# A hybrid decoder layer in fp32: the second mixer matrix with 14 pairs by products over halves, gate weights fetched a tile ahead, value products in one piece

## The chip, the core and the metric

The program runs on one core of one Trainium2 chip. Five engines take part: TensorE (PE, with its weight loads PEld), VectorE (DVE), ScalarE (ACT), GpSimd (POOL) and SyncE (SP). SP does nothing here but issue DMAs; a few are issued by POOL and ACT. Every engine works through its own instructions in a fixed order, and semaphores keep the engines in step. The metric is the time of one execution on the device in microseconds. Engine loads and stretches come from one profiled execution.

## What is computed

One inference step of a decoder layer for 1024 prompt tokens and 32 sample tokens (T = 1056), all in fp32:

```python
h = rmsnorm(x)
p = h @ w_in       # -> q, k, v | conv input | z | a | b | gate_A | gate_B
o_a = stick_breaking(q, k, v)          # 8 heads of 64, strictly causal, no softmax
o_b = gated_delta(conv(u), z, a, b)    # 4 heads, 128 x 128 state
m = sigmoid(gate_A) * (o_a @ w_pa) + sigmoid(gate_B) * (o_b @ w_pb)
x = x + m @ w_o
x = x + relu(rmsnorm(x) @ w_up)**2 @ w_down     # 1024 -> 4096 -> 1024
y = rmsnorm(x)
# stick_breaking: z = q.k/8 + bias; weight of key j =
#   sigmoid(z_j) * product over later keys l of (1 - sigmoid(z_l)); then weights @ v
```

The caches of keys and values, the convolution rows and the delta states are returned too.

## The kernel before

Every dense product is made of three matmuls in a single-pass fp32 format: each operand is split into a rounded part (`hi`, copied by ACT) and the rest (`lo`, subtracted by DVE), and `dense` (lines 134 to 139) issues hi by hi (L137), hi by lo (L138) and lo by hi (L139) into one PSUM tile. The weights come from device memory by DMA into a staging tile, and `load_w` (L117) or the like makes the two parts.

An automatic planner orders the instructions. It plays the program on a model of the engines and places on each engine, at each moment, a ready instruction, earlier lines of the program first; `tc.high_priority()` lifts what is inside, and `tc.issue_after(ins)` keeps what is inside behind `ins` on the engine of `ins`. The order so found is fixed in the program: on the chip each engine keeps to it, and waits where its next instruction isn't ready.

The stages, with their places in the profiled execution:

- Norm, input products, the delta heads and the sample tokens (0 to about 618 us). The 16 gate tiles (8 column tiles of 128 for gate_A and gate_B) are made by `gate_steps` (L1047), which calls `proj_steps` (L232): four steps, one for each of four pieces of the tokens; the first step loads the weight tile (`ws_g`, one staging buffer; `wh_g` and `wl_g`, two buffers each). Eleven gate tiles are written in the program before attention, five as filling inside it.
- Attention (about 618 to 869 us). Blocks are (head, i): 128 queries by 128(i+1) keys, 64 blocks, heads 6 and 7 taking turns at the end. `scores` makes z on PE (`sc`), the sigmoid on ACT, the causal mask (L951) and 1 - s (`am`, L954) on POOL, the running product (`pr`, a scan, L958) and its product with s (L959) on DVE. `stage_b` (L1030) then turns the weights by PE transposes (`wt`, L111) in PSUM, copies them out on ACT (L970), and `values_of` (L983) multiplies them by the values (`po`). For heads 0 to 5 two neighbouring blocks share one PSUM tile, one in rows 0 to 63 and one in rows 64 to 127, and the product of each step of 128 keys is issued for the one and then for the other, so `values_of` does something at odd i alone; heads 6 and 7 share one in the same way. Each value product takes 64 columns of the array and appears in the trace as two instructions. `pipeline` runs the scores LAG = 4 blocks ahead of the transposes and hands out the filling: the last five gate tiles and the transposes of x (`residual_step`) in the first 34 blocks, the products with w_pb (`pb_step`) in the other 30.
- Merge (`pa`) and output product with w_o (`px`), about 869 to 1008 us, then the norm ahead of the mixer.
- First mixer matrix (`pu`, about 1008 to 1350 us). The token columns are handled in two groups g. Of the 32 column tiles of w_up, tile f and tile f + 16 are a pair. A pair can be made plainly (`up_plain`, 8 row tiles deep), or with seven half-deep products over halves instead of eight (`up_weights`, `up_products`), which takes sums of weight quarters and of input quarters beforehand and sums of products behind. In group 0 the first NPL = 3 pairs are plain, which gives the input sums time to be made; all else goes by seven products.
- Second mixer matrix (`pw`, about 1350 to 1621 us). The hidden tiles f and f + 16 are a pair again. Pairs 3 to 15 go by seven products over halves, in three groups of 4, 4 and 5 pairs; `weight_part` (L1481) makes the weight sums and the hi and lo parts of each of the seven, `load_h` brings the hidden sums. Those were made at the end of `up_products` by four subtractions (L1410 to L1413) and written to `hc_d`, the squared hidden tiles of pairs 0 to 2 to `h_d`. For the first product of the first group the loads are issued by POOL, all the others by SP.
- Plain rest (`pv`, about 1621 to 1700 us): the six hidden tiles of pairs 0 to 2, in four stages of token columns, eight column tiles each, followed by the last norm, transposes (`fin`) and the stores.

Of the kernel before, what the change touches and what calls it, by code (L numbers as in the profile page):

```python
# [8 lines left out]
F32 = mybir.dt.float32  # L9
# [3 lines left out]
AF = mybir.ActivationFunctionType  # L13
ALU = mybir.AluOpType
# [4 lines left out]
P = 128  # L19
# [19 lines left out]
def hybrid_step(ctx, tc, x_prompt, x_sample, cache_k, cache_v, page_table, state_conv, state_ssm,  # L39
# [68 lines left out]
    V.memset(powc[:, 1:2], 0.5)  # L108

    def tr(out, in_, k=P):  # L110
        PE.transpose(out, in_, ident[:k, :k])  # L111

    def rpow(out, in_, which, n):
        G.tensor_tensor(out, in_, powc[: out.shape[0], which:which + 1].to_broadcast([out.shape[0], n]), op=ALU.pow)
# [114 lines left out]
                      [xhc[c][:, k] for k in range(KT)], [xlc[c][:, k] for k in range(KT)], n)  # L229
                evac(c, o, n, pt)  # L230

    def proj_steps(col, name, evac, done):  # L232
        ws = []

        def step(c, o, n):
            if not ws:
                ws.append(load_w(winv[:, :, col:col + P], name))
            wh, wl = ws[0]
            pt = dtile(f"pd_{name}_{c}", True)
            dense(pt, [wh[:, k] for k in range(KT)], [wl[:, k] for k in range(KT)],  # L240
                  [xhc[c][:, k] for k in range(KT)], [xlc[c][:, k] for k in range(KT)], n)
            evac(c, o, n, pt)
            if c == len(CX) - 1:
                done()

        return [lambda c=c, o=o, n=n: step(c, o, n) for c, (o, n) in enumerate(CX)]
# [692 lines left out]
    def scores(blk):  # L939
        hh, i = blk  # L940
        qs, kh, kl = heads[hh]
        n = P * (i + 1)
        qsl = slice(i * P, n)
        s = ak.tile([P, NP], F32, tag="s", name=f"s{hh}_{i}", bufs=LAG + 2)
        for k0 in range(0, n, 512):
            kn_ = min(512, n - k0)
            pt = dtile(f"sc{hh}_{i}_{k0}")
            PE.matmul(pt[:, :kn_], lhsT=qs[:, qsl], rhs=kh[:, k0:k0 + kn_], start=True, stop=False)
            last = PE.matmul(pt[:, :kn_], lhsT=qs[:, qsl], rhs=kl[:, k0:k0 + kn_], start=False, stop=True)
            S_.activation(s[:, k0:k0 + kn_], pt[:, :kn_], AF.Sigmoid, bias=sbb[:, hh:hh + 1], scale=HD ** -0.5)  # L950
        G.affine_select(s[:, qsl], s[:, qsl], pattern=[[-1, P]], compare_op=ALU.is_gt, fill=0.0, base=0,  # L951
                        channel_multiplier=1)
        am = ak.tile([P, NP], F32, tag="am", name=f"am{hh}_{i}", bufs=2)
        G.tensor_scalar(am[:, :n], s[:, :n], -1.0, 1.0, op0=ALU.mult, op1=ALU.add)  # L954

        pr = ak.tile([P, NP], F32, tag="pr", name=f"pr{hh}_{i}")
        am_r = am[:, n - 1:0:-1]
        V.tensor_tensor_scan(pr[:, n - 1:0:-1], am_r, am_r, 1.0, op0=ALU.mult, op1=ALU.bypass)  # L958
        V.tensor_tensor(s[:, :n - 1], s[:, :n - 1], pr[:, 1:n], op=ALU.mult)  # L959
        return s, last  # L960

    def transposed(blk, s):
        hh, i = blk
        wt = ak.tile([P, NP], F32, tag="wt", name=f"wt{hh}_{i}", bufs=2)
        for b0 in range(0, i + 1, 4):
            bn = min(4, i + 1 - b0)
            pt = ttile(f"wt{hh}_{i}_{b0}")
            for b in range(bn):
                tr(pt[:, b * P:(b + 1) * P], s[:, (b0 + b) * P:(b0 + b + 1) * P])
            S_.activation(wt[:, b0 * P:(b0 + bn) * P], pt[:, :bn * P], AF.Copy)  # L970
        return wt

    heads, vns, oTs, wts = {0: head0}, {}, {}, {}

# [55 lines left out]
    def stage_b(x, fill):  # L1030

        ahead = state[min(x + LAG, NB - 1)][1]
        with tc.issue_after(ahead.ins):
            wts[blks[x]] = transposed(blks[x], state[x][0])
        for f in fill:
            f()
        values_of(blks[x])

    def pipeline(x0, x1, fill):

# [7 lines left out]
    def gate_steps(j, b):  # L1048
        gt = fk.tile([P, T], F32, tag="ft", name=f"gt{b}_{j}", bufs=NFT)

        def ev(c, o, n, pt):
            with tc.high_priority():
                S_.activation(gt[:, o:o + n], pt[:, :n], AF.Sigmoid)

        return proj_steps(3592 + b * D + j * P, f"g{b}_{j}", ev, lambda: SY.dma_start((gA_d, gB_d)[b][j], gt))

    def residual_step(t):
        n = P if t < 8 else NS
# [172 lines left out]
    wuv = w_up[0].rearrange("(k p) n -> p k n", p=P)  # L1231
    wdv = w_down[0].rearrange("(k p) n -> p k n", p=P)
    h_d = dr.tile([FF // P, P, T], F32, name="h_d")
    NPL = 3
    hc_d = dr.tile([FF // P // 2 - NPL, 7, P, HN], F32, name="hc_d")

    def by_group(ap, g):
        return ap.rearrange("p (h g n) -> p g h n", h=2, g=2)[:, g]
# [100 lines left out]
    def next_bank(name):  # L1339
        bank[0] += 1  # L1340
        return mk4[bank[0] % 4](name)

    def up_plain(f, g):
        wh, wl = load_8(wuv[:, :, f * P:(f + 1) * P], f"up{f}")
        t = up_.tile([P, 7, QN], F32, tag="t", name=f"tp{f}{g}")[:, 0:2]
        for h, (i, ii) in enumerate(((0, 1), (7, 6))):
            pt = next_bank(f"pu{f}{g}_{h}")
            dense(pt, wh, wl, [Xh[g][i][:, k] for k in range(4)] + [Xh[g][ii][:, k] for k in range(4)],
                  [Xl[g][i][:, k] for k in range(4)] + [Xl[g][ii][:, k] for k in range(4)], QN)
            S_.activation(t[:, h], pt[:, :QN], AF.Relu)  # L1350
        S_.activation(t, t, AF.Square)
        SY.dma_start(by_group(h_d[f], g), t)

    def up_weights(f):
        a = wop.tile([P, 8, P], F32, tag="wh", name=f"ua{f}")
# [28 lines left out]
    def up_products(w7, f, g):  # L1384
# [22 lines left out]
            if f < NPL:  # L1407
                SY.dma_start(by_group(h_d[f + NF * r], g), rows[r])
        if f >= NPL:
            V.tensor_tensor(t[:, 4], t[:, 3], t[:, 0], op=ALU.subtract)  # L1410
            V.tensor_tensor(t[:, 3], t[:, 6], t[:, 3], op=ALU.subtract)
            V.tensor_tensor(t[:, 2], t[:, 6], t[:, 4], op=ALU.subtract)
            V.tensor_tensor(t[:, 5], t[:, 2], t[:, 1], op=ALU.subtract)  # L1413
            SY.dma_start(hc_d[f - NPL, :, :, g * QN:(g + 1) * QN].rearrange("i p n -> p i n"), t)

    out_proj(0)
    blocks(0)
# [10 lines left out]


    norm(1)  # L1430
    for f in range(NPL):
        up_plain(f, 0)
        up_plain(f + NF, 0)
    kxctx.close()
    u7a = pool("u7a", stack=uctx)
    for f in range(NPL, NF):
        w7 = up_weights(f)
        for g in range(2):
            up_products(w7, f, g)
        if f < 2 * NPL:  # L1440
            up_products(up_weights(f - NPL), f - NPL, 1)
    uctx.close()
    xg_ctx[1].close()
    woctx.close()
# [90 lines left out]
            last_q[0] = r if hasattr(r, "ins") else hq[0]  # L1535
        return r

    groups = [list(range(3, 7)), list(range(7, 11)), list(range(11, 16))]
    for gi, fs in enumerate(groups):
        qs2 = [quarters(f) for f in fs]  # L1540
        if gi:
# [3 lines left out]
        for i in range(7):  # L1545
# [9 lines left out]
            for n, f in enumerate(fs):  # L1555
                ld = lambda: load_h(hc_d[f - NPL, i], f"hc{f}_{i}", G if gi == 0 and i == 0 else SY)
                hs[n] = queued(ld) if gi == 0 and i else ld()
            ws = [weight_part(q, f, i) for q, f in zip(qs2, fs)]
            if gi == 0 and i == 0:
                ys[:] = [fp.tile([P, T], F32, name=f"y{j}") for j in range(KT)]  # L1560
            if gi == 0 and i in YLOAD:
# [116 lines left out]
```

## Time and profile before

| | us |
|---|---|
| runs | 1717.58, 1712.73, 1715.70 |
| median of the runs | 1715.7 |
| profiled execution | 1713.05 |
| its span, first to last instruction | 1711.3 |
| PE busy | 1676.0 |
| DVE busy | 1155.2 |
| ACT busy | 774.3 |
| POOL busy | 207.3 |

The share of busy time is that of the union of an engine's instructions. Matmuls overlap one another in the array: one of 264 columns is shown with about 284 ns from start to end, while the next one starts after less than half of it. So the work of PE is read from starts: the time from the first start to the last, divided by their number. A row of a timeline gives the start, the length and what was done; a row of the windows gives the busy time of each engine in a stretch.

### The profile page before, as it was taken

How to read it: one execution, taken by the hardware profiler on the slowest of the kernel's cores; microseconds unless marked ns; L12 is line 12 of the kernel's file. 1: busy time of each engine (PE TensorE's matmuls, PEld its weight loads, DVE VectorE, ACT ScalarE, POOL GpSimd, SP SyncE). 2: the span in 40 equal slices, each digit the busy share in tenths (PEclk: the TensorE clock that was granted, in tenths of full speed). 3: DMA queues.
4: the chain of work that ended last, by engine and by line, in shares of the span. 5: the costliest groups of instructions: out<-in, count | busy, mean ns of one | idle time of the engine just before them, and what ended most of it. 6: DMA issues, size and time to landing. Idle time of an engine off the chain costs nothing.

```text
span 1711.3 us, 34643 instructions
## 1 busy us (share of the span) xinstructions
PE 1676.0 (98%) x13958; PEld 1620.3 (95%) x13958; DVE 1155.2 (68%) x2317; ACT 774.3 (45%) x1542; POOL 207.3 (12%) x243
## 2 busy tenths in 40 slices
PE   6999999999999999999999999999999999999998
PEld 6999999999999799988999999999999999999998
DVE  6656676877325337779766578877777679788843
ACT  5453434343324225565433356544444564444353
POOL 1110111110004225345300000000000000000000
PEclk9999999999999999999999999999999999999999
DMA  5132233244537577876134645554443766433421
GB/s 181 38 118 81 69 95 103 73 124 134 152 96 233 156 202 181 201 211 189 44 126 132 176 132 150 160 160 145 139 139 125 268 216 214 144 118 96 133 78 62
DMA packets 259036, 239.24 MB, mean 140 GB/s; under 512 B 55890, under 2 KB 217011, under 8 KB 258876
## 3 DMA queue, kind: packets, MB, share of 16 engines
q1 hardware_dynamic: 253926, 226.27, 44.0%
q0 software_dynamic: 3200, 10.52, 2.0%
q8 instruction: 110, 1.80, 0.4%
q10 hardware_dynamic: 1750, 0.23, 0.1%
q14 instruction: 50, 0.41, 0.1%
HBM read 163.21 MB, written 73.77 MB: 138 GB/s over the span
## 4 chain that ended last, share of the span: by engine, by line
PE 88%; DVE 4%; DMA 4%; issue 2%; ACT 2%; SPq 0%; POOL 0%; DVEq 0%; POOLq 0%; ACTq 0%
PE pu L139 6%; PE pu L137 6%; PE pu L138 6%; PE pw L139 5%; PE pw L138 5%; PE pw L137 5%; PE pd_g L137 4%; PE pd_g L138 4%; PE pd_g L139 4%; PE wt L111 2%; PE po L996 2%; PE px L138 1%; PE px L137 1%; PE px L139 1%; PE pv L139 1%
## 5 line engine op out<-in xcount | busy, mean ns | idle before, releaser
L139 PE MATMUL pu<-Xh,ul 128*128 128x264 f32 x812 | 230.1, 284 | 0.0
L137 PE MATMUL pu<-Xh,uh 128*128 128x264 f32 x812 | 229.8, 283 | 0.1
L138 PE MATMUL pu<-Xl,uh 128*128 128x264 f32 x812 | 229.7, 283 | 0.0
L137 PE MATMUL pw<-hc,w 128*128 128x264 f32 x728 | 204.1, 284 | 2.4 <-ACT w L1490 2.4
L138 PE MATMUL pw<-hc,w 128*128 128x264 f32 x728 | 204.6, 285 | 0.0
L139 PE MATMUL pw<-hc,w 128*128 128x264 f32 x728 | 200.8, 285 | 1.0 <-DVE w L1491 1.0
L137 PEld LDWEIGHTS pu<-Xh,uh 128*128 128x128 f32 x812 | 153.1, 189 | 0.3 <-ACT uh L1241 0.3
L138 PEld LDWEIGHTS pu<-Xl,uh 128*128 128x128 f32 x812 | 152.7, 188 | 0.0
L139 PEld LDWEIGHTS pu<-Xh,ul 128*128 128x128 f32 x812 | 152.0, 188 | 0.0
L138 PE MATMUL pd_g<-xl,wh_g 128*128 128x256 f32 (+1 forms) x512 | 149.4, 292 | 0.0
L137 PE MATMUL pd_g<-xh,wh_g 128*128 128x256 f32 (+1 forms) x512 | 149.3, 292 | 0.0
L139 PE MATMUL pd_g<-xh,wl_g 128*128 128x256 f32 (+1 forms) x512 | 148.5, 290 | 0.0
L137 PEld LDWEIGHTS pw<-hc,w 128*128 128x128 f32 x728 | 136.8, 188 | 2.6 <-ACT w L1490 2.6
L138 PEld LDWEIGHTS pw<-hc,w 128*128 128x128 f32 x728 | 136.2, 188 | 0.0
L139 PEld LDWEIGHTS pw<-hc,w 128*128 128x128 f32 x728 | 134.4, 188 | 1.4 <-DVE w L1491 1.4
L958 DVE TENSOR_TENSOR_SCAN pr<-am 128x127 f32<-128x127 f32 (+7 forms) x64 | 89.0, 1393 | 30.1 <-POOL am L954 30.1
L137 PEld LDWEIGHTS pd_g<-xh,wh_g 128*128 128x128 f32 x512 | 97.1, 190 | 3.2 <-issue 2.5
L138 PEld LDWEIGHTS pd_g<-xl,wh_g 128*128 128x128 f32 x512 | 97.1, 190 | 2.7 <-issue 2.4
L139 PEld LDWEIGHTS pd_g<-xh,wl_g 128*128 128x128 f32 x512 | 97.0, 189 | 2.0 <-issue 1.8
L1490 ACT ACTIVATE w<-a 128x512 fp32r<-128x512 f32 x78 | 43.4, 620 | 90.3 <-PE pw L139 80.1
L139 PE MATMUL px<-mh,wl_wo 128*128 128x264 f32 x256 | 72.2, 285 | 1.3 <-DVE wl_wo L1242 1.2
L138 PE MATMUL px<-ml,wh_wo 128*128 128x264 f32 x256 | 72.6, 285 | 0.0
(578 smaller groups left out, 5069.0 us busy)
## 6 DMA issues: line engine op xcount, KB each, us to landing
hc_d<-t SPq DMA_DIRECT2D x26, 924.0 KB
hc<-hc_d SPq DMA_DIRECT2D x87, 264.0 KB
a<-in_w_down_dram SPq DMA_DIRECT2D x48, 256.0 KB
ws_g<-in_w_in_dram SPq DMA_DIRECT2D x16, 512.0 KB
ws_wo<-in_w_o_dram SPq DMA_DIRECT2D x32, 256.0 KB
ua<-in_w_up_dram SPq DMA_DIRECT2D x16, 512.0 KB
ub<-in_w_up_dram SPq DMA_DIRECT2D x16, 512.0 KB
gA_d<-gt SPq DMA_DIRECT2D x8, 528.0 KB
```

The source lines that it names most:

```text
L111: PE.transpose(out, in_, ident[:k, :k])
L137: PE.matmul(pt[:, :n], lhsT=wh[k], rhs=xh[k], start=(k == 0), stop=False)
L138: PE.matmul(pt[:, :n], lhsT=wh[k], rhs=xl[k], start=False, stop=False)
L139: PE.matmul(pt[:, :n], lhsT=wl[k], rhs=xh[k], start=False, stop=(k == nk - 1))
L958: V.tensor_tensor_scan(pr[:, n - 1:0:-1], am_r, am_r, 1.0, op0=ALU.mult, op1=ALU.bypass)
L996: PE.matmul(po[64 * r:64 * r + 64, 0:P], lhsT=vn[:, b, rs], rhs=wts[hh, 2 * m + r][:, b * P:(b + 1) * P], start=(b == 0), stop=(b == 2 * m ...
L1490: S_.activation(tl[:, 0], src, AF.Copy)
```

## The change

1. Second mixer matrix: 14 pairs by seven products (groups of 4, 5 and 5, from pair 2), two plain pairs in place of three. The first matrix keeps three plain pairs in group 0 (NPU), so pair 2, plain in group 0, makes its hidden sums there (`combos`). The weight parts of the very first product get high priority.
2. Gate weights: the first step of a gate tile, having split its own weights, issues the load of the next tile's.
3. Value products: those of block x - 1 are traced behind the last transpose of block x, in place of those of block x behind its filling. The turned weights get three buffers, the running product one in place of two.

```diff
-        PE.transpose(out, in_, ident[:k, :k])
+        return PE.transpose(out, in_, ident[:k, :k])
...
+    ahead_w = {}
+
+    def fetch_w(col):
+        ahead_w[col] = wpool.tile([P, 8, P], F32, tag="wst", name=f"ws_c{col}", bufs=1)
+        SY.dma_start(ahead_w[col], winv[:, :, col:col + P])
...
-                ws.append(load_w(winv[:, :, col:col + P], name))
+                if col not in ahead_w:
+                    fetch_w(col)
+                ws.append(load_w(None, name, st=ahead_w[col]))
+                if next_col is not None:
+                    fetch_w(next_col)
...
-        pr = ak.tile([P, NP], F32, tag="pr", name=f"pr{hh}_{i}")
+        pr = ak.tile([P, NP], F32, tag="pr", name=f"pr{hh}_{i}", bufs=1)
...
-        wt = ak.tile([P, NP], F32, tag="wt", name=f"wt{hh}_{i}", bufs=2)
+        wt = ak.tile([P, NP], F32, tag="wt", name=f"wt{hh}_{i}", bufs=3)
...
-                tr(pt[:, b * P:(b + 1) * P], s[:, (b0 + b) * P:(b0 + b + 1) * P])
+                last = tr(pt[:, b * P:(b + 1) * P], s[:, (b0 + b) * P:(b0 + b + 1) * P])
...
-            wts[blks[x]] = transposed(blks[x], state[x][0])
+            wts[blks[x]], last = transposed(blks[x], state[x][0])
+
+        if x:
+            with tc.issue_after(last.ins):
+                values_of(blks[x - 1])
         for f in fill:
             f()
-        values_of(blks[x])
+        if x == NB - 1:
+            values_of(blks[x])
...
-    NPL = 3
+
+    NPU, NPL = 3, 2
...
+    def combos(f, g, t):
+        V.tensor_tensor(t[:, 4], t[:, 3], t[:, 0], op=ALU.subtract)
+        V.tensor_tensor(t[:, 3], t[:, 6], t[:, 3], op=ALU.subtract)
+        V.tensor_tensor(t[:, 2], t[:, 6], t[:, 4], op=ALU.subtract)
+        V.tensor_tensor(t[:, 5], t[:, 2], t[:, 1], op=ALU.subtract)
+        SY.dma_start(hc_d[f - NPL, :, :, g * QN:(g + 1) * QN].rearrange("i p n -> p i n"), t)
...
     def up_plain(f, g):
...
+        rows = (t[:, 0:4:3], t[:, 1:7:5])
+        for r in range(2):
+            wh, wl = load_8(wuv[:, :, (f + NF * r) * P:(f + NF * r + 1) * P], f"up{f}{r}")
...
+            if f < NPL:
+                SY.dma_start(by_group(h_d[f + NF * r], g), rows[r])
+        if f >= NPL:
+            combos(f, g, t)
...
-    for f in range(NPL):
+    for f in range(NPU):
         up_plain(f, 0)
-        up_plain(f + NF, 0)
...
-    groups = [list(range(3, 7)), list(range(7, 11)), list(range(11, 16))]
+    groups = [list(range(2, 6)), list(range(6, 11)), list(range(11, 16))]
...
-            ws = [weight_part(q, f, i) for q, f in zip(qs2, fs)]
+            with tc.high_priority() if gi == i == 0 else ExitStack():
+                ws = [weight_part(q, f, i) for q, f in zip(qs2, fs)]
```

More of the change, by code (lines that the diff above doesn't have):

```diff
@@ L230, in proj, with proj_steps @@
                 evac(c, o, n, pt)
-    def proj_steps(col, name, evac, done):
+    ahead_w = {}
+    def fetch_w(col):
+        ahead_w[col] = wpool.tile([P, 8, P], F32, tag="wst", name=f"ws_c{col}", bufs=1)
+        SY.dma_start(ahead_w[col], winv[:, :, col:col + P])
+    def proj_steps(col, name, evac, done, next_col=None):
         ws = []
@@ L968, in transposed @@
             for b in range(bn):
-                tr(pt[:, b * P:(b + 1) * P], s[:, (b0 + b) * P:(b0 + b + 1) * P])
+                last = tr(pt[:, b * P:(b + 1) * P], s[:, (b0 + b) * P:(b0 + b + 1) * P])
             S_.activation(wt[:, b0 * P:(b0 + bn) * P], pt[:, :bn * P], AF.Copy)
-        return wt
+        return wt, last
     heads, vns, oTs, wts = {0: head0}, {}, {}, {}
@@ L1053, in ev, with col @@
                 S_.activation(gt[:, o:o + n], pt[:, :n], AF.Sigmoid)
-        return proj_steps(3592 + b * D + j * P, f"g{b}_{j}", ev, lambda: SY.dma_start((gA_d, gB_d)[b][j], gt))
+        def col(j, b):
+            return 3592 + b * D + j * P
+        return proj_steps(col(j, b), f"g{b}_{j}", ev, lambda: SY.dma_start((gA_d, gB_d)[b][j], gt),
+                          None if (j, b) == (KT - 1, 1) else col(*((j, 1) if b == 0 else (j + 1, 0))))
     def residual_step(t):
@@ L1341, in next_bank @@
         return mk4[bank[0] % 4](name)
-    def up_plain(f, g):
[L1344 to L1352, printed above, removed]
+    def combos(f, g, t):
[4 more added lines that the diff above has]
+        SY.dma_start(hc_d[f - NPL, :, :, g * QN:(g + 1) * QN].rearrange("i p n -> p i n"), t)
+    def up_plain(f, g):
+        t = up_.tile([P, 7, QN], F32, tag="t", name=f"tp{f}{g}")
+        rows = (t[:, 0:4:3], t[:, 1:7:5])
+        for r in range(2):
+            wh, wl = load_8(wuv[:, :, (f + NF * r) * P:(f + NF * r + 1) * P], f"up{f}{r}")
+            for h, (i, ii) in enumerate(((0, 1), (7, 6))):
+                pt = next_bank(f"pu{f}{g}{r}_{h}")
+                dense(pt, wh, wl, [Xh[g][i][:, k] for k in range(4)] + [Xh[g][ii][:, k] for k in range(4)],
+                      [Xl[g][i][:, k] for k in range(4)] + [Xl[g][ii][:, k] for k in range(4)], QN)
+                S_.activation(rows[r][:, h], pt[:, :QN], AF.Relu)
+            S_.activation(rows[r], rows[r], AF.Square)
+            if f < NPL:
+                SY.dma_start(by_group(h_d[f + NF * r], g), rows[r])
+        if f >= NPL:
+            combos(f, g, t)
     def up_weights(f):
@@ L1409, in up_products @@
         if f >= NPL:
[L1410 to L1414, printed above, removed]
+            combos(f, g, t)
     out_proj(0)
@@ L1430, in hybrid_step @@
     norm(1)
-    for f in range(NPL):
+    for f in range(NPU):
         up_plain(f, 0)
-        up_plain(f + NF, 0)
     kxctx.close()
     u7a = pool("u7a", stack=uctx)
-    for f in range(NPL, NF):
+    for f in range(NPU, NF):
         w7 = up_weights(f)
@@ L1439, in hybrid_step @@
             up_products(w7, f, g)
-        if f < 2 * NPL:
-            up_products(up_weights(f - NPL), f - NPL, 1)
+        if f < 2 * NPU:
+            up_products(up_weights(f - NPU), f - NPU, 1)
     uctx.close()
```

## The prediction

> **What bounds the kernel now.** I read the page first, its loads and its chain, and then the windows, stretch by stretch.
>
> ```profile
> span 1711.3 us, 34643 instructions
> PE 1676.0 (98%) x13958; PEld 1620.3 (95%) x13958; DVE 1155.2 (68%) x2317; ACT 774.3 (45%) x1542; POOL 207.3 (12%) x243
> ...
> PE 88%; DVE 4%; DMA 4%; issue 2%; ACT 2%; SPq 0%; POOL 0%; DVEq 0%; POOLq 0%; ACTq 0%
> ```
>
> PE is idle for 1711.3 - 1676.0 = 35 us, and 88% of the chain that ends last is PE. So a saving must come out of PE's own order: fewer instructions, or a cheaper sequence of them. But PE is also shown busy where it only takes what others let through, so I ask of each stretch who else is full. The windows of the stretches that matter (columns: length, PE, PEld, DVE, ACT, POOL busy, clock, DMA):
>
> ```profile
> 1034.00:1052.00 18.00, 18.00 (x150) 18.00 (x149) 18.00 (x28) 13.25 (x26) 0.00 (x0) 1.00 0.47 142
> 1052.00:1064.00 12.00, 11.93 (x99) 11.72 (x98) 10.70 (x19) 8.19 (x16) 0.00 (x0) 1.00 0.78 208
> 762.00:798.00 36.00, 34.25 (x263) 28.72 (x264) 34.62 (x32) 20.70 (x40) 24.89 (x20) 1.00 0.88 250
> 745.00:762.00 17.00, 17.00 (x138) 14.10 (x138) 10.76 (x12) 10.95 (x25) 5.43 (x8) 1.00 0.62 182
> 618.00:745.00 127.00, 126.99 (x1035) 116.05 (x1034) 87.28 (x84) 62.18 (x138) 52.30 (x70) 1.00 0.84 199
> 798.00:869.00 71.00, 71.00 (x613) 63.63 (x612) 45.69 (x67) 29.19 (x64) 19.49 (x30) 1.00 0.16 50
> ```
>
> In attention DVE has room from 618 to 745 (87.28 of 127) and from 798 to 869 (45.69 of 71), but none from 762 to 798 (34.62 of 36). From 745 to 762 DVE is not full either, but the chain of waits leaves PE there:
>
> ```profile
> 761.92 2.02 DVE pr L958
> 763.94 1.13 DVE obl L1137
> ```
>
> Here the last filling gates are used up, and the next filling can't start before a split that stands behind scans on DVE. What PE saves between 745 and 798 I count as lost.
>
> **Value products in one piece.** The timeline of PE around one of them, a block with i = 7 (start, length, instruction, count):
>
> ```profile
> 666.08 1.03 PE L111 MATMUL wt<-ident,s 128*128 128x128 f32 x8
> 667.05 0.43 PE L996 MATMUL po<-wt,vn 128*64 128x128 f32 x2
> 667.41 0.50 PE L948 MATMUL sc<-kh,qs 128*128 128x512 f32 x1
> ...
> 669.88 0.28 PE L139 MATMUL pd_g<-xh,wl_g 128*128 128x256 f32 x1
> 670.08 1.96 PE L996 MATMUL po<-wt,vn 128*64 128x128 f32 x28
> 671.98 0.55 PE L111 MATMUL wt<-ident,s 128*128 128x128 f32 x3
> ```
>
> The first step of the product, which needs only the older block's turned weights, is taken at once; the other 28 instructions come three microseconds later, when the younger block's have been copied. That costs twice. First, the two blocks use different halves of the array's columns and work side by side: 28 instructions take 671.98 - 670.08 = 1.90 us, 68 ns each, while the two that went alone hold PE for 667.41 - 667.05 = 0.36 us. The older block has 7 steps, the younger 8, each of two instructions. With one step gone ahead, the 28 are 12 pairs and 4 alone, 16 places; all 30 together are 14 pairs and 2 alone, 16 places as well. So the 0.36 us go away whole. Second, the change from dense matmuls into value products costs time: the dense one before the 28 holds PE for 670.08 - 669.88 = 0.20 us, against 0.12 us of its neighbours (worked out below for the mixer), 0.08 us. After the change the values of block x - 1 are bound to come behind the last transpose of x; both of their operands were copied a block earlier, and they are traced ahead of the filling, so nothing keeps them apart. Each group then has one entry, from a transpose, as the first piece has now. I take 0.36 + 0.08 = 0.44 us for a group.
>
> ```profile
> 640.11 0.43 PE L996 MATMUL po<-wt,vn 128*64 128x128 f32 x2
> ...
> 745.00 0.43 PE L996 MATMUL po<-wt,vn 128*64 128x128 f32 x2
> ...
> 789.14 0.43 PE L996 MATMUL po<-wt,vn 128*64 128x128 f32 x2
> ...
> 864.02 0.43 PE L1010 MATMUL po<-wt,vn 128*64 128x128 f32 x2
> ...
> 640.00:870.00 230.00, 53.94 (x576) 38.49 (x576) 2.28 (x8) 8.81 (x32) 1.00 0.60 155
> ```
>
> There are 32 groups (six heads with four, eight shared by heads 6 and 7), and each has such a first piece: in the timeline, from the first row above to the fourth, 32 of them. Eight lie between 745 and 798, the second row the first and the third the last of these. The last row is the window with the value products alone. All 32 give 14.1 us, the 24 outside give 10.6. I take **-10.6 us**, bounds -14.1 and 0. What the cover costs when gone: the turned weights are now read a block later, hence three buffers; `transposed` of x + 1 then waits for the values of x - 2 at most, which are behind it. One buffer for the scan loses nothing I can see, since scan and product are neighbours on one in-order engine. The stores of `oT` move one block later, and are read only after attention.
>
> **Fourteen pairs.** A pair costs 7 x 4 x 2 x 3 = 168 matmuls by products over halves (products, column tiles, token halves, three terms), and 2 x 8 x 4 x 3 = 192 plainly (two hidden tiles, column tiles, stages, terms). So 24 of 264 columns go.
>
> ```profile
> L137 PE MATMUL pw<-hc,w x728: 279/284/389, 1352.7 to 1620.8; 128*128 128x264 f32 x182
> ...
> L139 PE MATMUL pw<-hc,w x728: 278/285/393, 1354.8 to 1621.0; 128*128 128x264 f32 x182
> ```
>
> The length of 284 ns is not the price, for they overlap: 3 x 728 = 2184 matmuls start from 1352.7 to 1621.0; less the 1.0 us of waiting below, 267.3 / 2184 = 122 ns. 24 x 0.122 = **-2.9 us**. PE does nothing else for a pair; ACT and DVE take over one more pair of splits, in a stage where the third group ran five pairs already and no wait of PE shows behind 1388. In the plain rest the eight loads of weights fall from twelve, which takes away its only waits:
>
> ```profile
> L139 PE MATMUL pv<-hp,wd 128*128 128x264 f32 x192 | 54.7, 285 | 0.3 <-DVE wd L1599 0.3
> ```
>
> With the 0.2 us on L137 that is **-0.5 us**, at worst 0.
>
> In return pair 2 takes four subtractions more in group 0, between 1034 and 1064, where DVE is full by the windows above.
>
> ```profile
> L1410 DVE TENSOR_TENSOR t<-t x26: 423/432/435, 1071.0 to 1352.2; 128x264 f32<-128x264 f32 x26
> ```
>
> 4 x 0.43 = 1.7 us on DVE, ahead of the splits of the first seven products' weights. DVE has 12 - 10.70 = 1.3 us free behind 1052. Between 0 and 1.7, I take **+0.7 us**. The four for group 1 come where DVE has room.
>
> **The start of the second matrix.**
>
> ```profile
> 1349.36 0.65 ACT L1405 ACTIVATE t<-t 128x528 f32<-128x528 f32 x1 [5.03 <-DVE t L1401]
> ...
> 1352.04 1.14 ACT L1490 ACTIVATE w<-a 128x512 fp32r<-128x512 f32 x2
> ...
> 1352.71 0.39 PE L137 MATMUL pw<-hc,w 128*128 128x264 f32 x1 [2.40 <-ACT w L1490]
> ...
> 1384.75 0.39 PE L139 MATMUL pw<-hc,w 128*128 128x264 f32 x1 [0.51 <-DVE w L1491]
> ...
> 1388.44 1.25 PE L139 MATMUL pw<-hc,w 128*128 128x264 f32 x8 [0.50 <-DVE w L1491]
> ...
> 1364.44 0.69 DVE L1483 TENSOR_TENSOR s<-a,a 128x512 f32<-128x512 f32 x1 [3.27 <-DMA a<-in_w_down_dram]
> ...
> 1353.94 0.37 SPq L1414 DMA_DIRECT2D hc_d<-t  x1
> ```
>
> ACT idles for 5.03 us and then makes the last hidden squares ahead of the first weight part, and PE waits 2.40 us. With high priority that part goes into the idle time, if the planner's model has the weights landed. But what is late next shows already: from 1366 DVE is busy without a gap until PE waits for it twice, 0.51 and 0.50 us. DVE starts there when the quarters land (1364.44), and these are issued behind the last store of the hidden sums (1353.94), which high priority doesn't hasten, and delays if the four parts' `lo` go first. PE would reach the wait at 1384 2.4 us earlier and stand there longer; only evacuations that then fit DVE's idle 3.27 us before 1364 help. Between -2.4 and +2.8 (four `lo` of the size of L1483, 0.69, ahead of the store), I take **-1.2 us**.
>
> **Gate weights.**
>
> ```profile
> 470.18 1.23 DVE L128 TENSOR_TENSOR wl_g<-ws_g,wh_g 128x1024 fp32r<-128x1024 f32 x1 [1.68 <-ACT wh_g L127]
> ...
> 471.43 0.38 SPq L123 DMA_DIRECT2D ws_g<-in_w_in_dram  x1
> ...
> 659.02 1.52 DVE L128 TENSOR_TENSOR wl_g<-ws_g,wh_g 128x1024 fp32r<-128x1024 f32 x1
> ...
> 660.57 0.38 SPq L123 DMA_DIRECT2D ws_g<-in_w_in_dram  x1
> ```
>
> The load of the next tile goes out in the same 0.1 us in which the split frees the one staging buffer: the planner fetches a tile ahead already. The buffer stays one, so the load can't go earlier: **0**, but for its place in SP's order (a rival).
>
> **Sum.** -10.6 - 2.9 - 0.5 + 0.7 - 1.2 = -14.5; the profiled execution took 1713.05, so 1698.6. The runs' median, 1715.7, lies 2.65 above it, and from there it would be 1701.2. I say **1700 us**, own range 1694 to 1706. About 0.3%, 5 us, is what a measurement of this kernel can tell from no change.
>
> **Rivals.**
>
> *DVE and POOL, not PE, set the pace of all attention.* For it: the chain from 745 on; DVE and POOL together are busy 87.28 + 52.30 = 139.6 us of 127 from 618 to 745. Were they unable to overlap at all, no PE saving would count. Against: they sum to more than the stretch, so they do overlap, and from 798 to 869 they sum to only 65 of 71. Then the 10.6 are lost: 1713.05 - 2.9 - 0.5 + 0.7 - 1.2 = 1709. [...] Chance 0.14.
>
> *The pieces stay apart*, because the planner still takes dense matmuls between them: half the gain, 1704. Chance 0.08.
>
> *All 32 groups count, and the start of the second matrix too*: 1713.05 - 14.1 - 2.9 - 0.5 - 2.4 = 1693. Chance 0.08.
>
> *Slower: SP stands behind the fetch.* SP issues in order. A fetch that is placed earlier in it waits for the split that frees the buffer, and the loads of the next head's keys wait behind. How tight these are:
>
> ```profile
> PE sc L948 <- DMA kh<-kh_d: 0.8, 1, 0.8
> ...
> 655.80 0.33 SPq L1055 DMA_DIRECT2D gB_d<-gt  x1
> ```
>
> Before 660.57 SP stood 4.4 us for the fetch, harmlessly. If each of the five fetches in attention held up a head's loads by that, it would be +22, and the time 1721; it decides from about 14.5 / 4.4, more than three of five. Against it: scores run four blocks ahead, and only one wait for keys shows. Chance 0.08.
>
> The forecast keeps 0.62. Faster by over 0.3%: 0.62 + 0.08 + 0.08, and 0.01 of the first rival, 0.79; within: 0.13; slower: 0.08. The range goes from 1691 to 1710: it takes in three of the rivals and the unknown terms, and leaves out the slower one.
>
> **What would show it.** Right: 32 value pieces of PE in place of 64, and their window at about 53.94 - 32 x 0.43 = 40 us; the stretch from the first scores to the merge, 618 to 869, some 10 us shorter; 2352 `pw` and 384 `pv` matmuls at 122 ns; ACT's first weight part ahead of the last squares; waits at the third and fourth product longer than 0.5. Wrong: attention as long as before with PE waiting for `am`, scans or sigmoids; `sc` waiting for `kh`; `pu` waiting for splits at 1055. The forecast is wrong if the planner's new order, which is one plan for the whole program, opens a wait that no row of before shows.

## Result and profile after

The changed kernel takes 1701.9 us (median of 8 runs, 1698.0 to 1708.4) beside 1714.2 us of the kernel before on the same chip (8 runs, 1711.2 to 1717.6): a ratio of 0.9931, 95% interval 0.9915 to 0.9948. The profiled execution took 1701.33 us, of which 1699.6 are the span. The head of its page and the shares of its chain:

```profile
span 1699.6 us, 34650 instructions
...
PE 1665.5 (98%) x13934; PEld 1616.3 (95%) x13934; DVE 1170.7 (69%) x2335; ACT 778.5 (46%) x1548; POOL 220.7 (13%) x243
...
PE 89%; DVE 4%; issue 2%; DMA 2%; POOL 1%; ACT 1%; SPq 0%; DVEq 0%; POOLq 0%; ACTq 0%
```

PE still bounds it; it has 10.5 us less to do. DVE is busy 15.5 us longer, with 18 instructions more; POOL is busy 13.4 us longer with the same 243 instructions as before. That is the first hint: POOL's rows get longer by what runs beside them.

Where the 11.7 us of span went is read from the first and the last matmul of each tile. First the kernel before, then after (count, shortest/median/longest ns, first to last start in us, shapes):

```profile
L948 PE MATMUL sc<-kh,qs x96: 221/387/504, 608.4 to 851.9; 128*128 128x512 f32 x48, 128*128 128x128 f32 x16, 128*128 128x256 f32 x16, 128*128 128x384 f32 x16
...
L137 PE MATMUL pb<-obh,wh_pb x128: 274/283/397, 762.9 to 868.8; 128*128 128x256 f32 x96, 128*128 128x288 f32 x32
...
L139 PE MATMUL pb<-obh,wl_pb x128: 278/283/362, 765.3 to 869.1; 128*128 128x256 f32 x96, 128*128 128x288 f32 x32
...
L137 PE MATMUL pv<-hp,wd x192: 278/283/390, 1621.2 to 1699.8; 128*128 128x264 f32 x192
...
L139 PE MATMUL pv<-hp,wd x192: 278/284/389, 1621.4 to 1700.0; 128*128 128x264 f32 x192
```

```profile
L958 PE MATMUL sc<-kh,qs x96: 219/387/775, 606.1 to 841.1; 128*128 128x512 f32 x48, 128*128 128x128 f32 x16, 128*128 128x256 f32 x16, 128*128 128x384 f32 x16
...
L137 PE MATMUL pb<-obh,wh_pb x128: 274/283/415, 754.5 to 860.2; 128*128 128x256 f32 x96, 128*128 128x288 f32 x32
...
L139 PE MATMUL pb<-obh,wl_pb x128: 274/283/417, 758.3 to 860.4; 128*128 128x256 f32 x96, 128*128 128x288 f32 x32
...
L137 PE MATMUL pw<-hc,w x784: 278/284/422, 1344.6 to 1633.3; 128*128 128x264 f32 x196
...
L137 PE MATMUL pv<-hp,wd x128: 278/284/371, 1633.6 to 1687.7; 128*128 128x264 f32 x128
...
L139 PE MATMUL pv<-hp,wd x128: 279/284/290, 1633.9 to 1687.9; 128*128 128x264 f32 x128
```

From such rows:

| stretch | before | after | difference |
|---|---|---|---|
| ahead of the first scores | 608.4 | 606.1 | -2.3 |
| first scores to first `pb` (gates fill) | 154.5 | 148.4 | -6.1 |
| first to last `pb` (merge of branch b fills) | 106.2 | 105.9 | -0.3 |
| last `pb` to first `pu` | 145.3 | 145.3 | 0.0 |
| first to last `pu` | 335.6 | 336.2 | +0.6 |
| last `pu` to first `pw` | 2.7 | 2.7 | 0.0 |
| first `pw` to last `pv` | 347.3 | 343.3 | -4.0 |
| behind it | 11.3 | 11.7 | +0.4 |

The first line is not the change's: up to the first scores both traces show the same instructions in the same order on every engine, but for one operation of DVE that changes its place even between two runs of the changed kernel. And that kernel has its first scores at 613.7 on another chip (e5). What is left is 6.1 us in the first part of attention, next to nothing in its second part, and 4.0 us in the second mixer matrix.

The timeline of PE around a value product after, and the window of all value products:

```profile
682.93 0.28 PE L138 MATMUL pd_g<-xl,wh_g 128*128 128x256 f32 x1
683.05 0.93 PE L111 MATMUL wt<-ident,s 128*128 128x128 f32 x7
683.90 1.53 PE L1006 MATMUL po<-wt,vn 128*64 128x128 f32 x22
685.37 0.39 PE L139 MATMUL pd_g<-xh,wl_g 128*128 128x256 f32 x1
...
640.00:870.00 230.00, 43.91 (x576) 34.48 (x576) 2.29 (x8) 8.98 (x32) 0.99 0.64 167
```

All 22 instructions come in one run, straight behind a transpose. The window falls from 53.94 to 43.91 us. Counted in the timeline, PE takes the value products in 39 unbroken pieces in place of 64; up to 773 there is no lone pair of instructions left, from there on there are seven.

PE's waits after (in all, times, longest):

```profile
PE xtp L111 <- DVE sst__148 L198: 10.1, 2, 9.9
PE pb L138 <- DVE obl L1156: 2.7, 2, 2.1
PE pw L137 <- ACT w L1517: 2.4, 1, 2.4
...
PE pb L137 <- DVE tb L1174: 1.0, 2, 0.8
```

The first stands before attention, in both kernels. The second was 0.2 us in the kernel before: at the turn from gates to `pb` PE waits for a split on DVE. The third is the wait that high priority was to shorten, as long as before. The split in the timeline, of the kernel before and then after, with POOL's row beside it:

```profile
763.86 1.20 DVE L1137 TENSOR_TENSOR obl<-ofb,obh 128x1024 fp32r<-128x1024 f32 x1
...
765.11 0.39 PE L138 MATMUL pb<-obl,wh_pb 128*128 128x256 f32 x1 [0.21 <-DVE obl L1137]
```

```profile
754.31 2.63 POOL L964 TENSOR_SCALAR am<-s 128x1024 f32<-128x1024 f32 x1
...
756.02 1.99 DVE L1156 TENSOR_TENSOR obl<-ofb,obh 128x1024 fp32r<-128x1024 f32 x1
...
758.06 0.38 PE L138 MATMUL pb<-obl,wh_pb 128*128 128x256 f32 x1 [2.11 <-DVE obl L1156]
```

DVE came earlier too, but not as much: the split begins 1.5 us behind the first `pb` where it was 0.9 (756.02 - 754.5, 763.86 - 762.9), and takes 0.8 us longer beside a pass of POOL that used to come behind it. PE has one product of scores to do in that gap in both kernels and stands for the rest of it: 0.9 us before (0.5 for `obh`, 0.2 for a sigmoid, 0.2 for `obl`), 2.3 after (0.2 for `obh`, 2.1 for `obl`). The windows over the turn (length; PE, PEld, DVE, ACT, POOL busy; clock; DMA) show what follows:

```profile
754.00:756.00 2.00, 1.79 (x14) 1.03 (x10) 1.99 (x1) 2.00 (x6) 1.91 (x2) 1.00 1.08 399
756.00:758.00 2.00, 0.00 (x0) 0.00 (x0) 2.00 (x3) 0.93 (x4) 2.00 (x2) 1.00 1.11 365
758.00:760.00 2.00, 1.94 (x12) 1.94 (x13) 2.00 (x3) 0.00 (x0) 1.91 (x3) 0.71 1.02 196
760.00:762.00 2.00, 2.00 (x10) 1.70 (x8) 2.00 (x2) 0.60 (x1) 2.00 (x2) 0.50 1.13 296
```

PE stands for 2 us, and then the granted clock is 0.5 for 3.4 us (758.8 to 762.2), which makes PE's work 1.7 us longer by my estimate (half of the 3.4). The same follows the wait for the first weight part at 1344 (0.5 from 1345.9 to 1349.3). The kernel before has its half-clock stretches at 17.6, 573.9 and 1707 only, none behind its own wait of 2.40 us at 1352.7. So the first theory was: the second part of attention lost its gain to a new wait and to the half clock behind it. The rival: DVE, full there, sets the pace, and what PE does between its waits is of no account.

### The profile page after: what moved, and what is told of

It reads as the page before. It is cut to its first block, busy times and chain, and to the rows that moved or that the text cites. A ratio compares the mean times of both kernels' runs of the same rounds, so it can differ in the third digit from the quotient of the medians.

```text
span 1699.6 us, 34650 instructions
## 1 busy us (share of the span) xinstructions
PE 1665.5 (98%) x13934; PEld 1616.3 (95%) x13934; DVE 1170.7 (69%) x2335; ACT 778.5 (46%) x1548; POOL 220.7 (13%) x243
## 4 chain that ended last, share of the span: by engine, by line
PE 89%; DVE 4%; issue 2%; DMA 2%; POOL 1%; ACT 1%; SPq 0%; DVEq 0%; POOLq 0%; ACTq 0%
PE pu L139 6%; PE pu L137 6%; PE pu L138 6%; PE pw L137 6%; PE pw L138 6%; PE pw L139 6%; PE pd_g L137 3%; PE pd_g L138 3%; PE pd_g L139 3%; PE wt L111 1%; PE px L138 1%; PE px L137 1%; PE px L139 1%; PE pd_uk L139 1%; PE po L1006 1%
## 5 line engine op out<-in xcount | busy, mean ns | idle before, releaser
L137 PE MATMUL pw<-hc,w 128*128 128x264 f32 x784 | 220.8, 285 | 2.8 <-ACT w L1517 2.4
L138 PE MATMUL pw<-hc,w 128*128 128x264 f32 x784 | 220.0, 286 | 0.0
L139 PE MATMUL pw<-hc,w 128*128 128x264 f32 x784 | 216.3, 286 | 0.0
L137 PEld LDWEIGHTS pw<-hc,w 128*128 128x128 f32 x784 | 148.1, 189 | 3.2 <-ACT w L1517 2.6
L138 PEld LDWEIGHTS pw<-hc,w 128*128 128x128 f32 x784 | 147.1, 189 | 0.0
L139 PEld LDWEIGHTS pw<-hc,w 128*128 128x128 f32 x784 | 145.7, 190 | 0.0
L968 DVE TENSOR_TENSOR_SCAN pr<-am 128x127 f32<-128x127 f32 (+7 forms) x64 | 89.5, 1399 | 19.1 <-POOL am L964 15.7
L1490 ACT ACTIVATE hc<-hc 128x528 fp32r<-128x528 f32 x98 | 62.1, 644 | 28.8 <-DMA hc<-hc_d 26.8
```

What stands on the lines that cost most here:

```text
L137: PE.matmul(pt[:, :n], lhsT=wh[k], rhs=xh[k], start=(k == 0), stop=False)
L138: PE.matmul(pt[:, :n], lhsT=wh[k], rhs=xl[k], start=False, stop=False)
L139: PE.matmul(pt[:, :n], lhsT=wl[k], rhs=xh[k], start=False, stop=(k == nk - 1))
L1490: S_.activation(tl[:, 0], tl[:, 1].bitcast(F32), AF.Copy)
```

## Experiments

Each ran beside the kernel before on its chip, in five rounds. The chips differ by up to 0.6% (medians of before 1711.6 to 1722.2), so ratios are compared, and lengths of stretches within a profile.

### The parts alone

e1 has only the value products behind the next block's transposes (with their buffers), e2 only the fourteenth pair with its high priority, e3 only the gate loads.

```diff
 e1: values_of(blks[x]) behind the filling -> values_of(blks[x - 1]) behind the last transpose; pr bufs=1, wt bufs=3
 e2: groups = [range(2, 6), range(6, 11), range(11, 16)]; NPU, NPL = 3, 2; combos; high priority
 e3: fetch_w(next_col) behind load_w in proj_steps
```

> The kernel before with the third part of the change alone (value products behind the next block's transposes, three buffers for turned weights, one for the scan). My theory: attention lost 6.3 us from the first scores to the last w_pb product in the changed kernel (260.6 to 254.4 us), all of it before 745 us; so 1 - 6.3/1714 = 0.996 of before, with 39 runs of value products on PE in place of 64. Rival: the 2.4 us that the changed kernel had gained before attention began belongs to this part too; then 0.995. Second rival: nothing of it reaches the end, ratio 1.000, and the gain of attention came from the gate weights.

> The kernel before with the first part alone (14 pairs, the high priority included). My theory: 4.0 us from the start of the second matrix to the last plain product, 0.6 us given back in the first matrix by the four subtractions; the first wait of the second matrix stays at 2.4 us. Ratio 1 - 3.4/1714 = 0.998. Rival: the two waits at the third and fourth product come back (1.0 us) without the shift from attention, ratio 0.9986.

> The kernel before with the second part alone (gate weights fetched a tile ahead). My theory: nothing changes, ratio 1.000 within 0.001; each load of a gate's weights is issued within 0.2 us of the split that frees its buffer, as before. Rival: it gives the 2.4 us by which attention began earlier, 0.9986; or it costs by standing in SP's queue ahead of the loads of keys, above 1.003.

Measured: e1 0.9970 (0.9959 to 0.9982), e2 0.9972 (0.9956 to 0.9988), e3 0.9993 (0.9984 to 1.0003). Their product is 0.9935, so the parts add up to the whole. On 1714.2 us the values are worth 5.1 us and the pairs 4.8; the gates nothing that can be told from zero. For the gates that is more than a small number: in the trace of e3 PE, DVE, ACT and POOL have the same instructions in the same order as in the kernel before, and on SP one load of gate weights (at 628.9 us) moves ahead of two other loads. What the high priority is worth by itself no run shows. The profile of e1 gains less in the first part than the whole change: 150.6 us from the first scores to the first `pb`, where e2 and e3 on the same chip have 154.2; it holds one wait of 1.8 us for ACT that the profile of after does not have.

### What took the second part's gain

e4 takes most of POOL's work away: 1 - s comes from ACT as the sigmoid of the negative argument, POOL keeps the diagonal tile.

```diff
+            S_.activation(am[:, k0:k0 + kf], pt[:, :kf], AF.Sigmoid, bias=nsbb[:, hh:hh + 1], scale=-(HD ** -0.5))
-        G.tensor_scalar(am[:, :n], s[:, :n], -1.0, 1.0, op0=ALU.mult, op1=ALU.add)
+        G.tensor_scalar(am[:, qsl], s[:, qsl], -1.0, 1.0, op0=ALU.mult, op1=ALU.add)
```

> The changed kernel with 1 - s made by ACT as the sigmoid of the negative argument straight from the scores, but for the diagonal tile of 128 keys, which POOL makes as before. It tells what bounds attention behind 745 us. My theory: the chain of POOL and DVE (POOL's pass, then the scan) does, so taking most of POOL's pass away (952 ns on average, 64 times) lets DVE start its scans earlier, DVE's idle time before scans falls from some 30 us to under 10, and attention gets 3 to 6 us shorter: ratio to before 0.990 or less. Rival: DVE's own work is the bound from 754 to 797, and it stays as long: ratio 0.993 as the changed kernel, or above it, since ACT has some 35 us more to do.

Measured: 0.9956 (0.9943 to 0.9969): no gain, and my expectation fell. The window of the first 53 us behind its first `pb`, and PE's waits there:

```profile
759.00:812.00 53.00, 48.24 (x375) 42.67 (x374) 42.11 (x45) 33.18 (x68) 13.28 (x24) 0.94 0.72 204
```

```profile
PE pb L137 <- ACT obh L1160: 1.9, 2, 1.3
PE pb L138 <- DVE obl L1161: 1.6, 1, 1.6
PE sc L961 <- DMA kh<-kh_d: 1.1, 1, 1.1
PE sc L961 <- ACT am L966: 0.8, 2, 0.5
```

POOL falls to 13.28 us and DVE to 42.11, and PE waits as long as ever, now for ACT, DVE and a load in turn. DVE's figure is lower mainly because less of its work falls into this window; over all of attention its scans, products and splits `obl` take 141 us, in after 150. Taking load off those two is not enough where the order of what is left makes PE wait.

e5 is the changed kernel again, as reference on one chip for e6 to e8.

> The changed kernel once more, as it is, so that the three runs beside it have a reference on the same chip. Both theories: a ratio of 0.993 to the kernel before, a PE wait of about 2 us for obl near 756 and of 2.4 us for the first weight part near 1344, each followed by 3.4 us at a granted clock of 0.5. If the half-clock stretch is chance and not a consequence of the wait, it lies elsewhere this time.

Measured: 0.9929 (0.9913 to 0.9944). The wait for `obl` is 3.6 us this time, and both half-clock stretches are there again, at 767.7 and 1354.8.

e6 makes `obl` on POOL.

```diff
-            V.tensor_tensor(obl[c], st, obh[c].bitcast(F32), op=ALU.subtract)
+            G.tensor_tensor(obl[c], st, obh[c].bitcast(F32), op=ALU.subtract)
```

> The changed kernel with the subtraction that makes obl (L1156) on POOL, out of the queue behind DVE's scans. My theory: the second part of the attention lost its gain because PE stood 2.1 us for obl and then ran 3.4 us at half clock, 1.7 us more; both go, the part from the first pb to the merge is 3 to 4 us shorter, and the ratio to the kernel before falls from 0.993 to 0.991. Rival (the second part is bound by DVE, whatever wakes PE): a wait of the same length comes at the next obl, tb or am, the half-clock stretch stays or moves by a few us, and the ratio stays at 0.993.

Measured: 0.9962 (0.9949 to 0.9975), slower than e5. A row of POOL's timeline and PE's waits at the turn say why:

```profile
767.86 7.48 POOL L1156 TENSOR_TENSOR obl<-ofb,obh 128x1024 fp32r<-128x1024 f32 x2
```

```profile
PE pb L137 <- DVE tb L1174: 5.4, 2, 5.1
PE pb L138 <- POOL obl L1156: 4.2, 1, 4.2
```

Two splits take 3.74 us each on POOL, against 1.3 to 2.0 on DVE, and hold up the next masks; the wait is 4.2 us, where it was 2.1 in after and 3.6 in e5, and the second part takes 113.8 us in place of e5's 107.4. The experiment does not decide between the theories, since the wait it was to remove grew.

e7 was made for the second matrix, and decided this question as well. It makes the last hidden squares on DVE.

```diff
+            if (f, g) == (NF - 1, 1):
+                V.scalar_tensor_tensor(rows[r], rows[r], 0.0, rows[r], op0=ALU.max, op1=ALU.mult)
```

> The changed kernel with the last hidden tile's relu and square as one operation of DVE in place of two of ACT, so that ACT can make the first weight part of the second matrix in its idle time. My theory: the wait of 2.4 us near 1344 and the 3.4 us at half clock behind it (1.7 us more) go, 2 to 4 us in all, ratio 0.991. Rival (what the prediction took to be late next): PE arrives at the third and fourth product 2 us earlier and waits there for DVE's weight parts; the ratio stays at 0.993.

Measured: 0.9924 (0.9909 to 0.9939) beside e5's 0.9929. The wait for ACT's first weight part is gone, and the half clock at 1345 with it. PE's waits from 1340 to 1400 in e7:

```profile
PE pw L139 <- DVE w L1521: 2.2, 2, 1.7
```

From the first `pu` to the first `pw` e7 needs 336.7 us in place of 338.9 after (1014.5 to 1351.2, 1005.7 to 1344.6), and from there to the last `pv` 344.0 in place of 343.3: 2.2 us come back as a wait for DVE's parts, less 1.7 us, by the same estimate, of half clock that no longer falls there. What is left, 1.5 us, lies within the intervals. The prediction's view that DVE is late next held.

In this run the half-clock stretch at the turn of attention did not come either, though PE waits 2.12 us for `obl` there as in the run of after. So the two profiles show the second part with and without it. The windows of 53 us behind the first `pb`: before, after, e7 (each in its own profile):

```profile
763.00:816.00 53.00, 51.25 (x411) 44.09 (x410) 48.62 (x48) 27.76 (x55) 33.16 (x28) 1.00 0.66 194
```

```profile
754.00:807.00 53.00, 49.04 (x384) 42.36 (x382) 50.31 (x46) 27.03 (x55) 31.66 (x28) 0.97 0.69 202
807.00:860.00 53.00, 53.00 (x483) 48.33 (x478) 34.16 (x55) 22.51 (x51) 15.36 (x23) 1.00 0.15 42
```

```profile
762.00:815.00 53.00, 47.47 (x384) 40.93 (x383) 50.32 (x46) 26.70 (x54) 32.38 (x27) 1.00 0.69 200
```

PE takes the same 384 instructions in both: in 49.04 us with the half clock, in 47.47 at full clock. The second part ends after 105.9 us in both, and the scans on DVE start within 0.02 us of the same places from block 39 on. e7's full clock bought only a longer wait: 4.4 us for `obl` in three places, in place of 2.7 in two. So the first theory is wrong in its second half: between these two profiles the half clock costs nothing, as DVE, busy for 50.3 of 53 us, hands out the next operands at the same moments. PE stands or crawls 53 - 47.5 = 5.5 us, against 1.75 before; that is 3.8 us, about what the whole pieces save in the second part (its value instructions take 19.7 us in place of 23.5, counted from start to start).

e8 moves DVE's product of s and the scan to POOL, with 1 - s on ACT (the scan back in two buffers, `oT` in one).

```diff
-        V.tensor_tensor(s[:, :n - 1], s[:, :n - 1], pr[:, 1:n], op=ALU.mult)
+        G.tensor_tensor(s[:, :n - 1], s[:, :n - 1], pr[:, 1:n], op=ALU.mult)
```

> The changed kernel with 1-s made by ACT (as in e4) and with the product of s and the scan moved from DVE to POOL, which takes some 10 us from DVE in the 44 us from 754 to 798 where it is full. If DVE's load sets the length of that stretch, it is 4 to 8 us shorter and the ratio falls to 0.989 or below. If the chain through scans and splits sets it (one block's latency, not the load), POOL's product is slower than DVE's and lies in that chain: the stretch is no shorter, and the ratio stays at 0.993 or rises.

Measured: 0.9997 (0.9984 to 1.0011): the whole gain is gone. PE waits 6.1 us for `am` of ACT and 4.2 for `obl`, and the first part takes 160 us (616.5 to 776.8). POOL's product is a link of each block's chain and slower there: 2.2 us on average for 1023 elements, against 1.4 on DVE in after. The experiment changes the load and this link at once, so it does not tell which of them counts.

e9 moves the turn two blocks on, so that `obl` falls among short scans.

```diff
-    SPLIT = 34
+    SPLIT = 36
```

> The changed kernel with the turn from gates to the first pb two blocks later (SPLIT 36), so that the splits obl (L1156) fall among scans of 127 to 383 elements instead of 767 to 1023. Theory A (DVE's pace around the turn took the second part's gain: 5.4 us of PE idle and half clock in the 53 us behind the first pb, against 1.8 before): the wait for obl falls under 1 us, the whole attention is 2 to 4 us shorter, ratio 0.991. Theory B (the second part's length is set elsewhere, by the last scans and what follows them): the wait goes and comes back as a wait for scans, tb or am; ratio 0.993.

Measured: 0.9968 (0.9953 to 0.9983), slower than the changed kernel. PE's waits from 755 to 812:

```profile
PE pb L138 <- DVE obl L1156: 4.7, 1, 4.7
PE pb L137 <- DVE tb L1174: 3.2, 2, 2.7
```

The wait grew from 2.1 to 4.7: the longest scan, of 1023 elements, still stood ahead of the split on DVE (758.72), which began at 763.81, 3.7 us behind the first `pb`. Both theories expected the wait to shrink; what sets it is where the planner puts the split, and moving the turn moved that too.

e10 leaves out seven of eight steps at most of the last sixteen blocks' value products, e11 the product of s and the scan from head 4's block 6 on.

```diff
 e10:
-        for b in range(i + 1):
+        for b in range(1):
 e11:
+        if hh < 5 and (hh, i) < (4, 6):
             V.tensor_tensor(s[:, :n - 1], s[:, :n - 1], pr[:, 1:n], op=ALU.mult)
```

> The changed kernel, in which the value products of heads 6 and 7 take only the first of their up to eight steps: 16 matmuls instead of 144 in the last 16 blocks, some 7 us of PE (144 to 16, 51 to 64 ns each). Theory A (DVE sets the pace only until about 807, PE behind it): nearly all of these blocks lie behind 797, so the 7 us come off the second part and the time. Theory C (DVE's scans set the pace to the end of attention): the last scans come at the same times, PE shows waits behind 797 that no row shows now, and under 3 us come off.

> The changed kernel without the product of s and the scan (L969) from head 4's block 6 on: that takes about 1 us a block, some 12 us of 44 in the stretch where DVE is full, off DVE, and one link out of the chain from score to value; PE's work is the same. Theory A: PE's idle time and half clock behind the first pb (3.8 + 1.7 us in the changed kernel) go nearly whole, the second part is 4 to 5 us shorter, ratio 0.990. Theory B or C, or PE alone: the waits move to other splits (tb, wl) and the ratio stays at 0.993.

Measured: e10 0.9933 (0.9907 to 0.9960), e11 0.9923 (0.9900 to 0.9947); on this chip e9 is 0.9968, and the changed kernel itself was not run there, so the lengths in the profiles decide. The windows of e10 and of e11 behind their first `pb`:

```profile
753.00:806.00 53.00, 48.27 (x370) 41.55 (x367) 50.25 (x46) 26.16 (x53) 31.73 (x27) 0.97 0.71 200
806.00:854.00 48.00, 47.29 (x375) 42.55 (x375) 33.09 (x53) 20.82 (x49) 17.73 (x24) 1.00 0.14 39
```

```profile
757.00:810.00 53.00, 50.73 (x411) 45.45 (x412) 36.27 (x34) 27.97 (x59) 21.65 (x28) 0.97 0.69 200
810.00:860.00 50.00, 50.00 (x447) 45.59 (x446) 24.59 (x42) 20.68 (x47) 9.85 (x21) 1.00 0.16 46
```

In e10 32 of the 144 value instructions of heads 6 and 7 are left; PE has 6.1 us less of them in the second part (13.6 in place of 19.7), and that part takes 101.0 us in place of 105.9 (753.2 to 854.3). So most of it comes off, as these blocks lie behind 806, where PE is full. In the first 53 us DVE's 50.25 and PE's 48.27 are nearly what they were. In e11 PE's work is the same, and DVE is busy 36.27 us there in place of 50.31; of the waits in the second part only 2.1 us for `obl` and 0.2 for `obh` are left, and that part takes 102.9 us (756.9 to 859.8), 3.0 less. Together the profiles say: for some 50 us behind the first `pb` DVE's side sets the pace, and after that PE. This rests on one profile of each. The runs don't show e10's 4.9 us: its ratio, 0.9933, is that of the changed kernel, its six runs go from 1695.1 to 1705.6, and the profiled one is the fastest of them. And e5, the changed kernel again, has 107.4 us for its second part, so some 1.5 us come and go without a change. Whether it is DVE's load or the link in each block's chain that counts is open: e11 takes both away, and e4, in which DVE's rows in all of attention get 9 us shorter, brought other waits in.

e12 combines e7 with value products two blocks behind (`wt` in four buffers, `oT` in one).

```diff
-        if x:
+        if x > 1:
...
-                values_of(blks[x - 1])
+                values_of(blks[x - 2])
```

> The changed kernel with the squares as in e7, the value products two blocks behind instead of one, and four buffers for the turned weights (one for oT). Seven lone pieces of two value instructions were left behind 773 in the changed kernel, 0.36 us each; the planned order has 36 pieces in place of 39. If a lone piece costs 0.36 to 0.44 us where PE is full (behind 807), up to three of them go, about 1 us, and with e7's 1 to 2 us the ratio is 0.991 to 0.992 against 0.993 for the changed kernel. Rival: turned weights that are read a block later shift the waits at the turn near 756 again, by a few us to either side, and that decides, as in e4 and e9: 0.994 or above.

Measured: 1698.7 us beside 1714.0, ratio 0.9906 (0.9883 to 0.9930), with 36 pieces. It has the lowest ratio of all versions, 0.7 to 1.2% below the kernel before; against the changed kernel, measured on other chips as 0.9931 and 0.9929, it gains some 0.2%, and the intervals overlap.

## Why the prediction was right, and where its steps were not

The time came out at 1701.9 where 1700 was said, and the two mechanisms that were to bring most of the gain, whole value products and a fourteenth pair, both brought some. That it came so close is partly luck. The sum forecast a gain of 14.5 us; the stretches that the change touches give 6.1 + 0.3 - 0.6 + 4.0 = 9.8 us in the profile, and the parts alone 5.1 + 4.8 = 9.9. The profile gained 2.3 us more ahead of the first scores, where the change does nothing, and the kernel before came out at 1714.2, 1.5 us below the median from which the prediction started. Two terms fell short, the value products by about 4 us and the start of the second matrix by 1.2; the pairs gave about 1 us more than said.

**Value products: the mechanism held, the count of groups that pay was too high.** Forecast -10.6 (24 groups of 0.44 us); e1 alone gives 0.30%, 5.1 us, and the profile -6.1 in the first part and -0.3 in the second. Forecast were 32 pieces and a window of about 40 us; 39 and 43.91 came. The price stands: in the kernel before, 15 lone first pieces lie ahead of the first `pb`, and 15 x 0.44 = 6.6. Counted from start to start, the value instructions there take 26.0 us for 296 before (88 ns each) and 21.5 for 308 after (70 ns); for 296 that is 5.3 us less, 0.35 a piece, where 0.36 was said. Three steps of the count failed. There are 29 lone pieces, not 32: at 675, 704 and 733 a group of six instructions went whole already. The four pieces from 745 to 762, which the prediction gave up, did pay: counted in PE's instructions since the first scores, the changed kernel leads by 5.8 us where the kernel before is at 742, and by 7.4 where it is at 760. And the ten behind 798, which it counted, paid nothing: five lone pieces are left there, and what the others save, with the pieces just ahead of them, is used up by the waits from 754 to 807. PE is full from there on in both kernels, but it enters that stretch with more of its work ahead.

**"DVE has no room from 762 to 798" was right, and reached too short.** DVE's fullness does not only cost the savings made within it. At the turn PE now reaches its wait for `obl` ahead of a later and slower split, and these 2.1 us are a wait that "no row of before shows", as the prediction's last point put it.

**Fourteen pairs.** Forecast -2.9 - 0.5 = -3.4; from the first `pw` to the last `pv` it is -4.0, and e2 alone gives 0.28%, 4.8 us. But the two profiles are not alike there. After has a half-clock stretch behind its first wait and none of the two waits for DVE's weight parts; the kernel before has these two waits, 1.0 us, and no half clock. Its wait of 2.40 us was spared by chance: e3, whose PE does the same in the same order, has such a stretch at 1357.7 and takes 348.5 us (1358.0 to 1706.5) in place of 347.3. Like with like, both with the stretch and the two waits, e2 takes 344.2 (1355.1 to 1699.3) against e3's 348.5, 4.3 us less; both without the stretch and with the two waits, e10 takes 342.8 (1339.0 to 1681.8) against 347.3, 4.5 us less. The mis-sized term is the one price of 122 ns for all matmuls. The plain rest falls from 78.8 to 54.3 us (1621.2 to 1700.0, 1633.6 to 1687.9); 0.5 of that are the waits that the prediction has in a term of its own, and the other 24.0 are 125 ns for each of the 192 matmuls that go. The 168 that come cost 20.0 us, 119 ns each, by e10 (288.5 us from the first `pw` to the first `pv`, 268.5 before).

**Four more subtractions**: +0.7 forecast, +0.6 from the first to the last `pu`; e7 and e12, the same there but for two operations, lie at 336.5 and 335.9, so the size is at the edge of what can be seen.

**Start of the second matrix**: -1.2 forecast, nothing came. With the high priority the weight part still stands behind the last squares (L1438) on ACT:

```profile
1343.38 0.64 ACT L1438 ACTIVATE t<-t 128x528 f32<-128x528 f32 x1
1343.93 1.13 ACT L1517 ACTIVATE w<-a 128x512 fp32r<-128x512 f32 x2
```

What the prediction said would be late next is what e7 met: 2.2 us of DVE's weight parts.

**Gates**: 0, and 0 it was.

**The rivals.** SP behind the fetch did not happen; PE shows no wait for keys in attention. That DVE and POOL set the pace of all attention is wrong for the first part, which gained 6.1 us, and right for half of the second.

## What to carry to other kernels

Here the saving on the busiest engine in attention paid 6.1 us ahead of the place where it had to meet a neighbour, the turn of the filling, and 0.3 us behind it; ask for each such place how much earlier the busy engine will arrive, and whether the neighbour can. Count the pieces to be saved one by one in the timeline, and price the instructions that go and those that come each by their own stretch, in profiles that are alike in waits and clock. A visible slowdown, such as a stretch at half clock, is not a cost until a run without it ends earlier; here the second part of attention took 105.9 us with it (after) and without it (e7).

## What the runs showed of the hardware

**Some short waits had half the clock behind them.** After waits of PE of 2.1 to 3.6 us the granted clock was 0.5 for 3.4 us in after and e5 (twice each), and was not after a wait of 2.12 us in e7 or of 2.40 in the kernel before. The wait of 2.4 us for the first weight part stands in twelve of the fourteen traces (not in e7 and e12), and in ten of them such a stretch goes with it (from 1345.9 in after, 1354.8 in e5, 1357.7 in e3; none in the kernel before and in e10). What decides whether it comes, no run shows.

**POOL's and DVE's rows were longer with more of the other's work beside them.** Rows of after and of e11 in the 53 us behind the first `pb`: shape and count, busy time, mean ns:

```profile
L961 POOL TENSOR_SCALAR_AFFINE_SELECT s<-s 128x128 f32<-128x128 f32 x14 | 15.7, 1124 | 18.1 <-ACT s L960 18.1
...
L964 POOL TENSOR_SCALAR am<-s 128x896 f32<-128x896 f32 x3 | 4.4, 1482 | 0.3
```

```profile
L961 POOL TENSOR_SCALAR_AFFINE_SELECT s<-s 128x128 f32<-128x128 f32 x14 | 7.2, 512 | 30.2 <-ACT s L960 25.9 <-DVE tb L1175 2.7 <-DVE pr L968 1.6
...
L964 POOL TENSOR_SCALAR am<-s 128x896 f32<-128x896 f32 x3 | 2.8, 941 | 0.3
```

The same fourteen masks take 15.7 us in the one and 7.2 in the other, and POOL as a whole 47.0 and 31.5 us in the second part, though only DVE lost work, its products of s and the scan. So the sum of 139.6 us of DVE and POOL in 127, which the prediction held against the first rival, proves nothing: a part of POOL's busy time goes with what DVE does beside it. The same is seen of DVE: in e4, with most of POOL's pass gone, the 64 products of s and the scan take 48.9 us on DVE, in after 53.4, and the four splits `obl` 5.2 us, in after 7.0. What makes the rows longer, and whether DVE and POOL were at work at the same time in them, no run shows.
